# A two-layer hybrid decoder trunk on one core: the first weight splits cut in two, the opening loads re-gated, and layer 1's squares added up on GpSimd

## The chip, the cores and the metric

The kernel runs on one core of a Trainium2 chip. The metric is device time in microseconds (us) of one execution. The core's engines run side by side and are named here as in the profile: PE is TensorE (matrix multiplications; PEld its weight loads), DVE is VectorE, ACT is ScalarE, POOL is GpSimd, SP is SyncE, which issues most of the loads and stores. Matmul results land in PSUM; everything else lies in SBUF, 128 partitions wide.

## What is computed

The reference carries a residual stream of 528 tokens (16 learned meta tokens, then 512 positions) by 1024 features through two layers, all in float32. Cut to what matters here:

```python
for l in range(DEPTH):                       # DEPTH = 2
    h = rmsnorm(h_res, norm_gain[l])
    proj = h @ w_in[l]
    u_pool, z_pool, c_q, c_kv, k_rope, z_mla, g_pool, g_mla = jnp.split(proj, IN_SPLIT_POINTS, axis=-1)
    y_pool = (pool_mix(u_pool, pool_w_group[l], pool_scale[l]) * jax.nn.silu(z_pool)) @ pool_w_up[l]
    o_mla = mla(c_q, c_kv, k_rope, pos, ...)           # c_q and c_kv are RMS-normed again; 8 heads, causal
    y_mla = (o_mla * jax.nn.silu(z_mla)) @ mla_w_up[l]
    merged = jax.nn.sigmoid(g_pool) * y_pool + jax.nn.sigmoid(g_mla) * y_mla
    h_res = h_res + merged @ w_out[l]
```

`rmsnorm` divides each token by the root of the mean of its squares over the 1024 features and multiplies each feature by a gain.

## The kernel before

**Layout.** Features lie on partitions and tokens along the free dimension, so the residual stream is eight tiles `xb[:, k]` of 128x528, k = 0 to 7. A product runs over the eight tiles as eight K steps, in two column halves of 264 tokens (`FULL`) in layer 0. In layer 1, whose meta tokens are needed only as keys and values, most products run over the 512 tokens at once (`XTOK`).

**Precision.** Each float32 operand is split into a rounded high part and a low remainder, and a product is three matmuls (`mm3`, L184 to L187): high weight by high data, high weight by low data, low weight by high data. For data the split is `split_h` (L333): ScalarE writes the high part `hh` with the norm's gain as scale (L337), VectorE the low part `hl` (L339). For weights it is `wload` (L170): a chunk of 128x512 (four K steps of 128 columns) comes into `raw`; ScalarE writes `whi` (L180), VectorE `wlo` (L181). The helper `split` (L275) does the same pair of instructions on any column range. The norm's division isn't in these operands: it is applied after the product, when the result leaves PSUM, with factors that are computed meanwhile.

**Norm sums.** `square_x` (L342) has ScalarE square each x tile (L344): in layer 0 after the first products, and in layer 1 for tile m as soon as layer 0's last product has written that tile (`ev_o`, L893, whose eviction is L903). `norm_sums` (L348) lets TensorE add these up across partitions with a matrix of ones, 32 columns wide: eight squares of x and two of the latent c_kv, by two column halves (L356). Four such matmuls stand side by side in the array, in four groups of 32 columns; x squares go alternately to two of them, and two partial sums come out, which are added after a trip through DRAM.

**Order of the work.** `register` (L914) lists the products of a layer in order: two of c_kv first, then c_q, u, keys and so on to the output product `o0` to `o7`. `stream` (L193) turns the list into chunks of 512 weight columns, with three to four loaded ahead, and exchanges the second and third chunk, so that the first four are: c_kv 0 K steps 0 to 3, c_kv 1 K steps 0 to 3, c_kv 0 K steps 4 to 7, c_kv 1 K steps 4 to 7. `step` (L238) advances it by a few matmuls, and `go` (L978) strings the layer together from such steps. The program's instructions are placed on the engines by a scheduler at compile time; each engine then runs its own list in order. `behind(a, b)` (L279) makes instruction a wait for b.

**The start.** The first chunk's load is issued on ScalarE's queue (L121) and named `first`. SP issues, in order, the norm scales `gn` (L122, 24 KB), x tile 0 (L123, 264 KB), the second chunk (L124, 256 KB) and x tile 1 (L125). `other_loads` (L141), called after tile 0's split, has SP load the rest behind `first`: x tiles 2 and 3 in one transfer (528 KB), the third chunk, tiles 4 and 5, the fourth chunk, tiles 6 and 7, the constants and the positions; weight chunks from the fifth on follow on the same queue (L114). Eight warm-up matmuls on a matrix of ones (L136) run on TensorE meanwhile. In `go`, layer 0 begins with this loop:

```python
for k in range(8):
    if k in (0, 1, 3, 5):
        step()                    # loads and splits the next chunk
    self.split_h(k)
    if k == 0:
        other_loads(first)
```

**The layer boundary.** `hh` and `hl` of layer 1 use the buffers that hold layer 0's merged result, the operand of `o0` to `o7`, so they are written while the last of these products finish. GpSimd has no work there; its next is an add for c_q (L563).

Of the kernel before, what the change touches and what calls it, by code (L numbers as in the profile page):

```python
# [9 lines left out]
F32 = mybir.dt.float32  # L10
# [3 lines left out]
AF = mybir.ActivationFunctionType  # L14
# [4 lines left out]
P = 128  # L19
# [4 lines left out]
T = SEQ + NM  # L24
# [11 lines left out]
MT_CKV = 0  # L36
# [35 lines left out]
def trunk(ctx, tc, xT, pos, win, wkr, wqb, wkb, wvb, wgr, wpu, wmu, wout, gains, const, yT):  # L72
# [45 lines left out]
        return wp.tile([P, 512], F32, tag="raw", name=nm("raw"), bufs=3)  # L118

    early.append(slot("rinv"))  # L120
    first = act.dma_start(early[0][:, 0:512], win[0, MT_CKV, :, 0:512])  # L121
    sp.dma_start(gn, gains)  # L122
    sp.dma_start(xb[:, 0, :T], xT[:, 0, :])  # L123
    early.append(fetch(win[0, MT_CKV + 1, :, 0:512], 512, rawt(), sp))  # L124
    sp.dma_start(xb[:, 1, :T], xT[:, 1, :])  # L125
# [13 lines left out]
    identr = cp.tile([P, P], F32R, name="identr")  # L139

    def other_loads(made):  # L141
        for k, m in ((2, 0), (4, 1), (6, None)):
            ins = sp.dma_start(xb[:, k:k + 2, :T], xT[:, k:k + 2, :])
            behind(ins, made)
            if m is not None:
                raw = rawt()
                behind(sp.dma_start(raw, win[0, MT_CKV + m, :, 512:1024]), made)
                early.append(raw)
        behind(sp.dma_start(cst, const), made)
        behind(sp.dma_start(posb[:, :T], pos.partition_broadcast(P)), made)  # L150
        dve.tensor_copy(maskw[:, 512 - P:], cst[:, C_MASK:C_MASK + P])
        dve.tensor_copy(identr, ident)
# [13 lines left out]
            self.spare = False  # L166

    loads = [0]

    def wload(src, n, gain, spare):  # L170
        raw = early.pop(0) if early else fetch(src, n, rawt(), sp)
        loads[0] += 1
        pool, th, tl, nb = (tp, "th", "tl", 2) if loads[0] <= 2 or spare else (wp, "whi", "wlo", 3)
        if gain is not None:
            v = raw[:, :n].rearrange("p (k m) -> p k m", k=8)
            gp.tensor_mul(v, v, gain.unsqueeze(2).to_broadcast([P, 8, n // 8]))
            return raw, None
        hi = pool.tile([P, W if pool is tp else 512], F32R, tag=th, name=nm("whi"), bufs=nb)
        lo = pool.tile([P, W if pool is tp else 512], F32R, tag=tl, name=nm("wlo"), bufs=nb)
        act.activation(hi[:, :n], raw[:, :n], AF.Copy)  # L180
        dve.tensor_sub(lo[:, :n], raw[:, :n], hi[:, :n].bitcast(F32))  # L181
        return hi, lo

    def mm3(out, wh, wl, xh, xl, start, stop):  # L184
# [94 lines left out]
    def behind(ins, other):  # L279
        tc.add_manual_dep(ins.ins, other.ins.name,  # L280
                          mybir.DependencyInfo(mybir.DependencyClass.Sync, mybir.DependencyReason.DATA))
# [32 lines left out]
    class Layer:  # L314
# [18 lines left out]
        def split_h(self, k):  # L333
            gk, x = self.g(G_H + k), self.xt[k]
            hh, hl = self.hs[k]
            for a, b in FULL if (self.l, k) == (0, 0) else [(0, T)]:
                made = act.activation(hh[:, a:b], x[:, a:b], AF.Copy, scale=gk)  # L337
                self.made[k] = self.made[k] or made
                dve.scalar_tensor_tensor(out=hl[:, a:b], in0=x[:, a:b], scalar=gk, in1=hh[:, a:b].bitcast(F32),  # L339
                                         op0=ALU.mult, op1=ALU.subtract)  # L340

        def square_x(self, k):  # L342
            self.xsq[k] = slot(f"cq{4 + k}" if k < 4 else f"q{k}")
            made = act.activation(self.xsq[k][:, :T], self.xt[k][:, :T], AF.Square)  # L344
            if self.l == 0:
                behind(made, self.made[min(k + 3, 7)])

        def norm_sums(self):  # L348
            fill_now(2600)
            px, pc = mmt(), mmt()  # L350
            runs = [(px, self.xsq[k], k, k < 2, k >= 6) for k in range(8)] + [(pc, self.csq[m], m, True, True) for m in range(2)]
            for k in range(0, 10, 2):
                for s, (a, b) in enumerate(FULL):
                    for ps, t, m, start, stop in runs[k:k + 2]:
                        g = 64 * s + 32 * (m % 2)
                        mm = pe.matmul(ps[g:g + 32, :HALF], ones[:, 0:32], t[:, a:b], start=start, stop=stop,  # L356
                                       tile_position=(0, g))
                        if t is not self.csq[1]:
                            behind(mm, self.csq_last)
            sums = tmp()  # L360
            for s, (a, b) in enumerate(FULL):
                act.activation(sums[0:64, a:b], px[64 * s:64 * s + 64, :HALF], AF.Copy)
                dve.tensor_copy(sums[64:128, a:b], pc[64 * s:64 * s + 64, :HALF])
            raw, norms = nsr[self.l], ndr[self.l]
            sp.dma_start(raw, sums[0:97:32, 0:T])
            C = T // 16
            parts = lambda d: d.rearrange("i (s c) -> s i c", c=C)
            fill_now(2600)
            nq = sm.tile([16, 4, C], F32, tag="nq", name=nm("nq"))
            na, nt, ny = (sm.tile([16, n, C], F32, tag=t, name=nm(t)) for t, n in (("na2", 2), ("nt2", 2), ("ny2", 3)))  # L370
            sp.dma_start(nq, parts(raw))
            dve.tensor_scalar(na[:, 0, :], nq[:, 0, :], 1.0 / D, EPS, op0=ALU.mult, op1=ALU.add)
            dve.scalar_tensor_tensor(out=na[:, 0, :], in0=nq[:, 1, :], scalar=1.0 / D, in1=na[:, 0, :],
                                     op0=ALU.mult, op1=ALU.add)
            dve.tensor_scalar(na[:, 1, :], na[:, 0, :], EPS, None, op0=ALU.mult)
            dve.tensor_scalar(ny[:, 2, :], na[:, 1, :], EPS, None, op0=ALU.mult)
            for m in range(2):
                dve.scalar_tensor_tensor(out=na[:, 1, :], in0=nq[:, 2 + m, :], scalar=1.0 / 256,
                                         in1=na[:, 1, :], op0=ALU.mult, op1=ALU.add)
            newton(ny[:, 0:2, :], na, nt)  # L380
            sp.dma_start(parts(norms), ny)
            self.inv, self.cinv = slot("rinv"), slot("q1")
            if self.l == 0:
                tables()
            fill_now(RET)
            for i, d in enumerate((self.inv, self.cinv)):
                behind(sp.dma_start(d[:, 0:T], norms[i:i + 1, :].partition_broadcast(P)), newest[0])
            self.st = [sct(), sct()]
# [589 lines left out]
        def go(self, nxt):  # L978
            l = self.l
            up = lambda name: upto((l, name))  # L980
            if l == 0:
                for k in range(8):
                    if k in (0, 1, 3, 5):
                        step()
                    self.split_h(k)
                    if k == 0:
                        other_loads(first)
            up("ckv1")
            if l == 0:
                for k in range(8):  # L990
                    self.square_x(k)
            self.norm_sums()
            up("u1")
            self.ninv = self.columns(1)
            for m in range(2):
                self.mix(m, self.window(m))
            up("u3")
            s2 = self.window(2)
            up("k3")
            s3 = self.window(3)  # L1000
            up("zp0")
            self.mix(2, s2)
            up("zp1")
            self.mix(3, s3)
            self.k_factors()
            self.eps = self.columns(2)
            up("qr1")
            for s, (a, b) in enumerate(FULL):
                a0 = max(a, self.x0)
                self.stat(self.acc[:, a0:b], a0, b, C_CQ, self.acc_last)  # L1010
            up("qn3")
            self.qk_stats()
            fill_now(2600)
            kq = self.prep(0)
            fill_now(2600)
            due[0] = None
            prev = None
            for h in range(H):
                kn_ = self.head(h, kq, prev)
                self.gap()  # L1020
                if h + 1 < H:
                    kq = self.prep(h + 1)
                self.pv(prev, (2, 3))
                prev = kn_
                self.gap()
            fill_now(1300)
            self.pv(prev, (0, 1))
            fill_now(2600)
            if not self.last:
                self.meta_queries()  # L1030
            self.pv(prev, (2, 3))
            up("gm7")
            flush()
            if not self.last:
                for p in range(4):
                    self.meta_out(p)
            up("o7")
            if nxt is not None:
                for k in range(8):
                    nxt.split_h(k)  # L1040
# [76 lines left out]
```

## Time and profile before

| | us |
|---|---|
| median of three timed runs | 787.66 |
| lowest and highest of them | 787.45, 788.19 |
| the profiled execution | 787.15 |
| its span in the profile | 785.4 |
| TensorE busy | 779.9 |
| VectorE busy | 536.7 |
| ScalarE busy | 410.9 |
| GpSimd busy | 195.5 |

The profile is of one execution. Its span runs from the first to the last instruction of the core; its time holds 1.75 us more, ahead of and behind the span. The granted clock of TensorE is 1.0 of full speed over the whole span. In rows of the timeline the first number is the start in us, the second the time until the end of the last instruction of the row (with xN for several); a bracket tells how long the engine stood idle before it and what ended that. Matmuls are pipelined, so one that takes 0.28 us may be followed by the next 0.12 us later. In rows that group instructions, the numbers behind the first bar are the total busy time in us and the mean of one in ns. A row of waits names who waited for whom, the total, how often, and the longest. A row of DMA issues ends with the median time from issue to landing.

### The profile page before, as it was taken

The numbers are of one execution on the slowest core, as the hardware profiler recorded it, in microseconds if no ns is written. First come the engines' busy times: TensorE is split into PE (matmuls) and PEld (weight loads), VectorE is DVE, ScalarE is ACT, GpSimd is POOL, SyncE is SP. The second block draws the span as 40 slices with busy tenths as digits, with TensorE's granted clock in tenths as the row PEclk, the third lists the DMA queues.
The fourth block names the chain that finished last, engine by engine and source line by source line (L and its number), as shares of the span: only waits on it lengthen the run. The fifth ranks groups of instructions, "written<-read, shape, count | busy, mean of one in ns | idle before, by whom it ended". The sixth has DMA issues, their size and how long they took to land.

```text
span 785.4 us, 14564 instructions
## 1 busy us (share of the span) xinstructions
PE 779.9 (99%) x5291; PEld 708.0 (90%) x5291; DVE 536.7 (68%) x1163; ACT 410.9 (52%) x930; POOL 195.5 (25%) x259
## 2 busy tenths in 40 slices
PE   9999999999999999999999999999999999999998
PEld 8999899999999999999997898887788888887887
DVE  5768778357779987685355577774477888755932
ACT  7645655555656565633354356455456666554421
POOL 1033504012333242052000235130132333410600
DMA  7233333323333222325642322434242323222372
GB/s 243 83 102 87 95 120 102 115 83 102 90 86 89 74 63 81 96 81 143 183 136 94 104 82 86 124 99 138 70 129 88 95 84 84 62 81 67 98 241 90
DMA packets 52983, 81.88 MB, mean 104 GB/s; under 512 B 9496, under 2 KB 18072, under 8 KB 52912
## 3 DMA queue, kind: packets, MB, share of 16 engines
q1 hardware_dynamic: 52768, 80.70, 33.8%
q8 instruction: 41, 0.67, 0.4%
q14 instruction: 30, 0.25, 0.1%
q10 hardware_dynamic: 144, 0.26, 0.1%
HBM read 74.51 MB, written 4.29 MB: 100 GB/s over the span
## 4 chain that ended last, share of the span: by engine, by line
PE 97%; DMA 1%; DVE 1%; ACT 0%; issue 0%; ACTq 0%
PE mm L185 29%; PE mm L187 28%; PE mm L186 28%; PE mm L801 2%; PE S L186 2%; PE S L187 2%; PE S L185 1%; PE o L807 1%; PE o L806 1%; PE S L456 1%; DMA xb<-xT 1%; PE mm L356 1%; PE mm L415 0%; DMA rinv<-win 0%; DMA raw<-wmu 0%; PE mm L812 0%
## 5 line engine op out<-in xcount | busy, mean ns | idle before, releaser
L185 PE MATMUL mm<-hh,whi 128*128 128x264 f32 (+2 forms) x1096 | 346.1, 317 | 0.5 <-ACT whi L180 0.3
L186 PE MATMUL mm<-hl,whi 128*128 128x264 f32 (+2 forms) x1096 | 343.7, 315 | 0.0
L187 PE MATMUL mm<-hh,wlo 128*128 128x264 f32 (+2 forms) x1096 | 342.6, 315 | 0.0
L181 DVE TENSOR_TENSOR wlo<-raw,whi 128x512 fp32r<-128x512 f32 (+2 forms) x251 | 188.7, 755 | 114.1 <-ACT whi L180 110.4
L180 ACT ACTIVATE whi<-raw 128x512 fp32r<-128x512 f32 (+2 forms) x251 | 150.1, 601 | 186.3 <-PE mm L186 129.8
L185 PEld LDWEIGHTS mm<-hh,whi 128*128 128x128 f32 x1096 | 205.7, 188 | 14.0 <-ACT racc L815 0.5
L186 PEld LDWEIGHTS mm<-hl,whi 128*128 128x128 f32 x1096 | 206.4, 188 | 11.8
L187 PEld LDWEIGHTS mm<-hh,wlo 128*128 128x128 f32 x1096 | 205.4, 188 | 12.1
L563 POOL TENSOR_TENSOR racc<-racc,tmp 128x264 f32<-128x264 f32 (+1 forms) x15 | 14.6, 978 | 151.7 <-ACT tmp L562 151.7
L704 POOL TENSOR_TENSOR tmp<-kp,bc 64x528 f32<-64x528 f32 x16 | 24.2, 1512 | 105.5 <-issue 90.0
L779 POOL TENSOR_TENSOR pm<-pa,rs 128x16 f32<-128x16 f32 x32 | 11.6, 361 | 149.8 <-DVE rs L774 149.8
L889 POOL TENSOR_TENSOR tmp<-tmp,xb 128x264 f32<-128x264 f32 (+1 forms) x24 | 27.0, 1150 | 58.5 <-DVE tmp L887 32.3
L735 DVE CUSTOM_DVE_ANT_0 S<-S,maskw,nqs 128x272 f32<-128x272 f32 (+4 forms) x80 | 38.4, 498 | 2.3 <-PE S L187 1.9
L742 ACT ACTIVATE cq<-S,bia 128x400 f32<-128x400 f32 (+2 forms) x48 | 24.6, 515 | 21.4 <-DVE bia L769 11.7
L185 PE MATMUL mm<-u,whi 128*128 128x264 f32 (+1 forms) x108 | 35.3, 327 | 0.0
L187 PE MATMUL mm<-u,wlo 128*128 128x264 f32 (+1 forms) x108 | 34.7, 321 | 0.0
L187 PE MATMUL mm<-cq,wlo 128*128 128x264 f32 (+1 forms) x108 | 34.6, 322 | 0.0
L185 PE MATMUL mm<-cq,whi 128*128 128x264 f32 (+1 forms) x108 | 34.6, 320 | 0.0
L186 PE MATMUL mm<-cq,whi 128*128 128x264 f32 (+1 forms) x108 | 34.5, 321 | 0.0
L277 DVE TENSOR_TENSOR tl<-mm,th 128x512 fp32r<-128x512 f32 (+1 forms) x64 | 29.2, 481 | 7.0 <-ACT th L276 6.3
L781 POOL TENSOR_TENSOR cq<-cq,rs 128x384 f32<-128x384 f32 (+1 forms) x32 | 33.0, 1030 | 0.0
L276 ACT ACTIVATE th<-mm 128x512 fp32r<-128x512 f32 (+1 forms) x64 | 25.4, 433 | 10.7 <-PE mm L801 10.4
(246 smaller groups left out, 1363.6 us busy)
## 6 DMA issues: line engine op xcount, KB each, us to landing
raw<-win SPq DMA_DIRECT2D x143, 256.0 KB, 2.6
raw<-wout SPq DMA_DIRECT2D x32, 256.0 KB, 3.1
bc<-kdr SPq DMA_DIRECT2D x16, 264.0 KB, 3.6
raw<-wpu SPq DMA_DIRECT2D x16, 256.0 KB, 2.7
raw<-wmu SPq DMA_DIRECT2D x16, 256.0 KB, 2.7
raw<-wqb SPq DMA_DIRECT2D x12, 256.0 KB, 2.6
tmp<-xT SPq DMA_DIRECT2D x16, 132.0 KB, 3.2
tmp<-scr SPq DMA_DIRECT2D x7, 256.0 KB, 3.0
```

Of the source, the lines that this page charges most:

```text
L180: act.activation(hi[:, :n], raw[:, :n], AF.Copy)
L181: dve.tensor_sub(lo[:, :n], raw[:, :n], hi[:, :n].bitcast(F32))
L185: pe.matmul(out, wh, xh, start=start, stop=False)
L186: pe.matmul(out, wh, xl, start=False, stop=False)
L187: newest[0] = pe.matmul(out, wl, xh, start=False, stop=stop)
L276: act.activation(hi[:, a:b], src, AF.Copy)
L277: dve.tensor_sub(lo[:, a:b], src, hi[:, a:b].bitcast(F32))
L704: gp.tensor_mul(kf[r0:r0 + 64, :], self.kp[r0:r0 + 64, :], bc[r0:r0 + 64, :])]
L735: dve.tensor_tensor_reduce(out=sv, in0=sv, in1=mask, scale=nqs[:, i, h:h + 1], scalar=3e38, op0=ALU.add, op1=ALU.min, accum_out=bia[:, c:c ...
L742: act.activation(pv, sv, AF.Exp, scale=-1.0, bias=bia[:, i:i + 1], accum_out=rs[:, c:c + 1])
L781: gp.tensor_mul(pt[i][:, NM:], pt[i][:, NM:], rs[:, i:i + 1].to_broadcast([P, n - NM]))
L889: gp.tensor_add(t[:, :b - a], t[:, :b - a], self.am[m][:, a:b])
```

## The change

- The first chunk's load is no longer the gate of the other loads; the load of the norm scales `gn` is.
- `other_loads` issues x tiles 2 to 7 one by one, with the third chunk behind tile 3 and the fourth behind tile 4.
- Of the first two chunks, `wload` splits columns 0 to 127 (K step 0) at once; the other 384 columns are split by a function kept in `rests`. That of the first chunk is called behind tile 0's split, that of the second behind tile 1's, and ScalarE's part of each waits for the high part of that tile (`made`, which now holds the last of the tile's two halves).
- In layer 1, `square_x` has GpSimd add up the squares: behind an odd tile the pair, behind tiles 3 and 7 the two pairs as well. The sums of tiles 0 to 3 and 4 to 7 lie in the first and fifth tile, and `norm_sums` takes these two in place of eight.

```diff
--- before.py
+++ after.py
@@ -118,8 +118,8 @@
         return wp.tile([P, 512], F32, tag="raw", name=nm("raw"), bufs=3)
 
     early.append(slot("rinv"))
-    first = act.dma_start(early[0][:, 0:512], win[0, MT_CKV, :, 0:512])
-    sp.dma_start(gn, gains)
+    act.dma_start(early[0][:, 0:512], win[0, MT_CKV, :, 0:512])
+    first = sp.dma_start(gn, gains)
     sp.dma_start(xb[:, 0, :T], xT[:, 0, :])
     early.append(fetch(win[0, MT_CKV + 1, :, 0:512], 512, rawt(), sp))
     sp.dma_start(xb[:, 1, :T], xT[:, 1, :])
@@ -139,12 +139,11 @@
     identr = cp.tile([P, P], F32R, name="identr")
 
     def other_loads(made):
-        for k, m in ((2, 0), (4, 1), (6, None)):
-            ins = sp.dma_start(xb[:, k:k + 2, :T], xT[:, k:k + 2, :])
-            behind(ins, made)
-            if m is not None:
+        for k in range(2, 8):
+            behind(sp.dma_start(xb[:, k, :T], xT[:, k, :]), made)
+            if k in (3, 4):
                 raw = rawt()
-                behind(sp.dma_start(raw, win[0, MT_CKV + m, :, 512:1024]), made)
+                behind(sp.dma_start(raw, win[0, MT_CKV + k - 3, :, 512:1024]), made)
                 early.append(raw)
         behind(sp.dma_start(cst, const), made)
         behind(sp.dma_start(posb[:, :T], pos.partition_broadcast(P)), made)
@@ -166,6 +165,7 @@
             self.spare = False
 
     loads = [0]
+    rests = []
 
     def wload(src, n, gain, spare):
         raw = early.pop(0) if early else fetch(src, n, rawt(), sp)
@@ -177,8 +177,14 @@
             return raw, None
         hi = pool.tile([P, W if pool is tp else 512], F32R, tag=th, name=nm("whi"), bufs=nb)
         lo = pool.tile([P, W if pool is tp else 512], F32R, tag=tl, name=nm("wlo"), bufs=nb)
-        act.activation(hi[:, :n], raw[:, :n], AF.Copy)
-        dve.tensor_sub(lo[:, :n], raw[:, :n], hi[:, :n].bitcast(F32))
+        first = P if loads[0] <= 2 else n
+        split(hi, lo, raw[:, 0:first], 0, first)
+        if first < n:
+            def rest(made):
+                behind(act.activation(hi[:, first:n], raw[:, first:n], AF.Copy), made)
+                dve.tensor_sub(lo[:, first:n], raw[:, first:n], hi[:, first:n].bitcast(F32))
+
+            rests.append(rest)
         return hi, lo
 
     def mm3(out, wh, wl, xh, xl, start, stop):
@@ -335,7 +341,7 @@
             hh, hl = self.hs[k]
             for a, b in FULL if (self.l, k) == (0, 0) else [(0, T)]:
                 made = act.activation(hh[:, a:b], x[:, a:b], AF.Copy, scale=gk)
-                self.made[k] = self.made[k] or made
+                self.made[k] = made
                 dve.scalar_tensor_tensor(out=hl[:, a:b], in0=x[:, a:b], scalar=gk, in1=hh[:, a:b].bitcast(F32),
                                          op0=ALU.mult, op1=ALU.subtract)
 
@@ -344,12 +350,19 @@
             made = act.activation(self.xsq[k][:, :T], self.xt[k][:, :T], AF.Square)
             if self.l == 0:
                 behind(made, self.made[min(k + 3, 7)])
+                return
+            for w in (1, 2):
+                if k % (2 * w) == 2 * w - 1:
+                    d, e = self.xsq[k - 2 * w + 1], self.xsq[k + 1 - w]
+                    gp.tensor_add(d[:, :T], d[:, :T], e[:, :T])
 
         def norm_sums(self):
             fill_now(2600)
             px, pc = mmt(), mmt()
-            runs = [(px, self.xsq[k], k, k < 2, k >= 6) for k in range(8)] + [(pc, self.csq[m], m, True, True) for m in range(2)]
-            for k in range(0, 10, 2):
+            xs = self.xsq[::4] if self.l else self.xsq
+            runs = [(px, t, m, m < 2, m >= len(xs) - 2) for m, t in enumerate(xs)]
+            runs += [(pc, t, m, True, True) for m, t in enumerate(self.csq)]
+            for k in range(0, len(runs), 2):
                 for s, (a, b) in enumerate(FULL):
                     for ps, t, m, start, stop in runs[k:k + 2]:
                         g = 64 * s + 32 * (m % 2)
@@ -982,9 +995,13 @@
                 for k in range(8):
                     if k in (0, 1, 3, 5):
                         step()
+                        if k == 1:
+                            rests.pop(0)(self.made[k - 1])
                     self.split_h(k)
                     if k == 0:
                         other_loads(first)
+                    if k == 1:
+                        rests.pop(0)(self.made[k])
             up("ckv1")
             if l == 0:
                 for k in range(8):
```

## The prediction

> **What bounds the kernel now.** I read the page first (busy time, and the shares of the chain that ended last), then what TensorE waits for, then that chain's first pieces in order of time, and last the two places that the diff touches.
>
> ```profile
> PE 779.9 (99%) x5291; PEld 708.0 (90%) x5291; DVE 536.7 (68%) x1163; ACT 410.9 (52%) x930; POOL 195.5 (25%) x259
> ...
> PE 97%; DMA 1%; DVE 1%; ACT 0%; issue 0%; ACTq 0%
> ```
> ```profile
> PE wps L136 <- DVE na L680: 1.0, 1, 1.0
> PE mm L185 <- ACT whi L180: 0.3, 1, 0.3
> ```
> ```profile
> 0.73 2.86 DMA rinv<-win
> 3.61 5.02 DMA xb<-xT
> 8.65 0.74 ACT hh L337
> 9.42 0.78 DVE hl L339
> 10.24 0.39 PE S L186
> ```
>
> The reader sees that TensorE is the bound: 779.9 us busy of a span of 785.4, 97% of the chain, and behind the first wait (1.0 us, ahead of the warm-up matmuls) none above 0.3 us. So time is won in two ways only: fewer matmuls, or an earlier moment from which TensorE never stands still. The chain names that moment. Ahead of 10.24 us it is not TensorE's: the first weight chunk lands at 3.59, this releases the load of x tiles 2 and 3, which lands at 8.63; ScalarE rounds tile 2, VectorE forms its low part until 10.20, and from 10.24 on it is matmuls.
>
> **The change part by part.** *Norm sums of layer 1.*
>
> ```profile
> 420.60 1.10 PE L356 MATMUL mm<-cq,ones 128*32 128x264 f32 x16
> ...
> 421.52 1.52 PE L356 MATMUL mm<-q,ones 128*32 128x264 f32 x24
> ...
> 422.96 0.50 PE L185 MATMUL mm<-hh,whi 128*128 128x512 f32 x1
> ```
>
> Ten tensors (eight squares of x, two of c_kv) by two column halves are 20 matmuls; the trace has 40 instructions, two to a matmul. They hold TensorE from 420.60 to 422.96: 2.36 us, 0.059 us an instruction. With four squares added up in each of two tensors, (2 + 2) x 2 x 2 = 16 instructions are left, in groups of four as before: 16 x 0.059 = 0.94 us. This takes 24 x 0.059 = **1.42 us** out of TensorE's queue where TensorE is the bound, so all of it counts. Layer 0 keeps its 40.
>
> What is added for it are six adds of 128x528 on GpSimd: one behind the square of tile 1, two behind tile 3's, one behind tile 5's, two behind tile 7's.
>
> ```profile
> L522 POOL TENSOR_TENSOR tmp<-u 128x542 f32<-128x542 f32 x3 | 4.7, 1563 | 6.3 <-DVE u L499 6.3
> ...
> L522 POOL TENSOR_TENSOR tmp<-u 128x528 f32<-128x528 f32 x1 | 1.1, 1066 | 0.9 <-DVE u L499 0.9
> ```
> ```profile
> 404.84 0.63 ACT L344 ACTIVATE q<-xb 128x528 f32<-128x528 f32 x1
> ```
> ```profile
> 431.60 1.33 POOL L563 TENSOR_TENSOR racc<-racc,tmp 128x512 f32<-128x512 f32 x1 [72.32 <-ACT tmp L562]
> ```
>
> By these rows an add costs 1.07 to 1.56 us, six 6.4 to 9.4. GpSimd has stood idle for 72 us when it starts at 431.60, so nothing waits behind the adds on its queue. The last square ends at 405.47, the two adds behind it by 407.6 to 408.6, and TensorE wants them at 420.60: 12 us of cover. I cost them at nothing; without that cover it would be the last two, 2.1 to 3.1 us. GpSimd may also slow VectorE beside it:
>
> ```profile
> 403.83 0.43 DVE L903 SCALAR_TENSOR_TENSOR xb<-mm,tmp 128x264 f32<-128x264 f32 x1
> ...
> 407.49 0.69 DVE L181 TENSOR_TENSOR wlo<-raw,whi 128x512 fp32r<-128x512 f32 x1
> ```
> ```profile
> 397.73 0.28 PE L185 MATMUL mm<-hh,whi 128*128 128x264 f32 x1
> ...
> 403.46 0.28 PE L187 MATMUL mm<-hh,wlo 128*128 128x264 f32 x1
> ```
>
> Between the last two rows lie 47 steps from matmul to matmul, so one takes 0.122 us. VectorE evicts layer 0's last tile at 403.83. TensorE then has two chunks of 24 matmuls (5.9 us, to about 409.6) before it needs the two chunks that VectorE finishes at 408.18. VectorE may thus slip 1.4 us at no cost.
>
> The Trainium skill (GPSIMD Engine Reference, § 1 and § 4.1) speaks against this part: an elementwise add of two inputs belongs on VectorE, as GpSimd is about twice as slow and shares its SBUF interface with VectorE's instructions that have two SBUF inputs. Where that would lead here is the third rival, priced from rows.
>
> *The start.*
>
> ```profile
> 1.18 0.41 SPq L123 DMA_DIRECT2D xb<-xT  x1
> ```
> ```profile
> 1.05 3.78 PE L136 MATMUL wps<-ones 128*128 128x128 f32 x16 [1.05 <-DVE na L680]
> ...
> 4.34 0.92 ACT L337 ACTIVATE hh<-xb,gn 128x264 fp32r<-128x264 f32 x2
> ...
> 5.77 0.63 ACT L180 ACTIVATE whi<-raw 128x512 fp32r<-128x512 f32 x1 [0.51 <-DMA raw<-win]
> ...
> 6.43 0.74 ACT L337 ACTIVATE hh<-xb,gn 128x528 fp32r<-128x528 f32 x1
> ...
> 7.20 0.77 DVE L339 SCALAR_TENSOR_TENSOR hl<-xb,gn,hh 128x528 fp32r<-128x528 f32 x1
> ...
> 13.82 1.36 ACT L337 ACTIVATE hh<-xb,gn 128x528 fp32r<-128x528 f32 x2
> ...
> 14.58 1.45 DVE L339 SCALAR_TENSOR_TENSOR hl<-xb,gn,hh 128x528 fp32r<-128x528 f32 x2 [0.52 <-ACT hh L337]
> ```
> ```profile
> xb<-xT SPq DMA_DIRECT2D x3, 528.0 KB, 5.0
> xb<-xT SPq DMA_DIRECT2D x2, 264.0 KB, 3.1
> ```
> ```profile
> 2.00:11.60 9.60, 9.01 (x53) 7.91 (x52) 5.02 (x8) 6.51 (x12) 1.62 (x6) 1.00 0.97 335
> 6.00:8.00 2.00, 1.72 (x14) 1.52 (x12) 1.46 (x2) 1.13 (x2) 0.00 (x0) 1.00 1.05 322
> 9.00:18.00 9.00, 8.76 (x70) 8.35 (x69) 6.52 (x11) 9.00 (x17) 0.00 (x0) 1.00 0.68 258
> 12.00:14.00 2.00, 2.00 (x18) 2.00 (x18) 2.00 (x5) 2.00 (x5) 0.00 (x0) 1.00 1.02 394
> ```
>
> (In the windows the last two columns are the DMA engines' busy share and GB/s, the one ahead the granted clock.) The two splits: ScalarE takes 0.46 us for a half of 264 columns (0.92 x2) and 0.74 for 528, so 0.0011 us a column; 128 columns cost about 0.3 us and the other 384 about 0.5, VectorE's pieces the same. Each chunk costs both engines 0.1 to 0.2 us more in all and frees its first piece 0.35 us sooner. For the first chunk that frees nothing: x tile 0 lands at 1.18 + 3.1 = 4.28 by a load that stays where it is, ScalarE begins it at 4.34 either way, and the warm-up matmuls hold TensorE until 4.83. The second chunk lands near 5.72 as now, so its matmuls begin at about 6.1 in place of 6.45. Tile 1 has landed by 6.43, as ScalarE goes straight on to it. I put it at 6.35: ScalarE has it by 7.1 and the second chunk's rest by 7.6, VectorE tile 1's low part by 7.9 and that rest by 8.45, and the 24 matmuls of tiles 0 and 1 are done at about 8.75.
>
> The other loads wait for the scales, not for the weight chunk at 3.59. No row shows the scales land. They are 24 KB, issued at 0.74 ahead of tile 0, which took 3.1 us with eleven times the bytes, and are used at 4.34; I take 3.2. The issue itself is worth little, from -0.2 to 0.4 us, as the DMA engines are 0.97 busy from 2.0 us on. What counts is that tile 2 no longer comes as one load with tile 3. Its 264 KB are 270 thousand bytes, at 322 GB/s 0.84 us: it lands at 8.63 - 0.84 = 7.8, with the issue's gain at 7.4. Three more DMA issues (0.41 us the row above) lengthen SP's queue by 1.2 us; behind them stand the constants, the positions and the fifth weight chunk, whose matmuls come behind 96 others (11.7 us): covered.
>
> With tile 2 at 7.7, ScalarE has it by 8.45 and VectorE its low part by 9.25. TensorE does its 24 matmuls until 8.75, four with tile 2's high part until 9.24, and then takes the low part, where it stood at 10.24 before: 1.0 us. By the load alone it is 0.84, and if tile 2 comes sooner still, tile 1's chain (8.75) holds it at 1.0. I take **0.9 us**. What is late next is ScalarE, busy throughout from 9 to 18 us: it rounds tiles 6 and 7 from 13.82 on, tile 6's low part is there at 14.58 + 0.73 = 15.3, and TensorE asks for it 48 matmuls behind 10.24, at 16.1. So 0.8 us are safe even if ScalarE's late tiles don't move; third and fourth chunk stand one tile earlier in the queue. Lower end 0.2, if squares are put ahead of tiles; upper end 1.6, if tile 1 comes sooner too.
>
> **The sum.** The profiled execution took 787.15 us, 785.4 of span and 1.75 around it: 787.15 - 1.42 - 0.9 = 784.83. The median of the three timed runs is 787.66, 0.51 higher; 787.66 - 2.32 = **785.3**. A difference of 0.2%, 1.6 us, is about what a measurement of this kernel can tell from no change.
>
> **The rivals.** (1) *The start gives little or nothing*: single loads move slower, or ScalarE's new order takes back what tile 2 gives. Against it: from 12 to 14 us, with the pairs through (9.6 us x 335 GB/s is 3.2 million bytes by 11.6 us, the last x tile among them), single loads run at 394 GB/s, the pairs' time has 322. For it: the compiled order of ScalarE's work is in no trace of before, and one square is 0.63 us. Only the norm sums stay: 787.66 - 1.42 = 786.2. Chance 0.18. The Trainium skill (DMA: Bandwidth & Descriptors, § Bandwidth) weighs on this side: it advises batches of 1 MiB or more. The windows just read don't agree for loads that overlap.
>
> (2) *A better start*: tile 1 lands sooner too, and the gain is 1.3 to 1.6 us: 784.7. Against it: its load stands where it did. Chance 0.1.
>
> (3) *GpSimd holds VectorE off at the layer boundary.* If the two exclude each other, VectorE slips by the last two adds, 2.1 to 3.1 us, of which 1.4 are covered: TensorE stalls 0.7 to 1.7, 786.0 to 787.0. For it: the splits stand right there. Against it: adds of this size differ by 0.5 us at most, so engines that meet slow each other by less than an instruction. Chance 0.06.
>
> (4) *Slower: the engines serve all loads in flight in parallel.* Then tile 2, released together with five tiles and two chunks, doesn't go first. At the worst all land together: their bytes have moved by 11.6 us, and landing comes some 1.3 later (the pair's 1.6 million bytes had moved by about 7.2 at 322 GB/s, and it landed at 8.63), at 12.9. TensorE starts 4.2 us later than now: 787.66 + 4.2 - 1.42 = 790.4. The point from which it decides is tile 2 landing later than 8.63 + 1.42 = 10.05. Against it: tile 0 landed at 4.28 with two later loads under way. Chance 0.06, as 788 to 790.5.
>
> **How the numbers follow.** The forecast has 0.6 (its own range 785.0 to 785.7), the rivals 0.18, 0.1, 0.06 and 0.06; predicted 785.3. Down to (2), up through (1) and part of (3), the range is 784.4 to 786.6. Faster by over 0.2% (below 786.1): the forecast, (2) and a bit under half of (1), 0.78. Within 0.2%: the rest of (1), (3) and a little of (4), 0.16. Slower: most of (4), 0.06.
>
> **What would show it.** Right would be: 16 matmul instructions in layer 1's norm sums, 0.94 us; six GpSimd adds ahead of 409 us and no TensorE wait for them; tile 2's rounding at 7.5 to 7.9 in place of 8.65; its first low-part matmul near 9.3, with no TensorE gap behind. Wrong would be a tile 2 that lands after 8.6, gaps of TensorE from 10 to 18 us, or a wait at the layer boundary.

## The result, and the profile after

The changed kernel takes 785.63 us (median of 12 runs, 785.29 to 787.55) against 787.43 for the kernel before (12 runs, 786.61 to 788.19): a ratio of 0.9979, interval 0.9972 to 0.9986, so 1.8 us less. Its profiled execution took 785.55 us with a span of 783.8; that of before had 787.15 and 785.4.

The page of the changed kernel, busy times and then the shares of the chain that ended last:

```profile
PE 778.4 (99%) x5267; PEld 707.5 (90%) x5267; DVE 541.0 (69%) x1165; ACT 411.0 (52%) x932; POOL 204.8 (26%) x265
...
PE 98%; DMA 1%; DVE 0%; ACT 0%; issue 0%; SPq 0%; ACTq 0%
```

TensorE has 24 instructions fewer and is still the bound. GpSimd is busy 9.3 us more, and VectorE 4.3 us more although it has only two short instructions more: something slows it. The changed kernel's chain, its first pieces in order of time:

```profile
0.74 0.39 SPq L122
1.19 3.14 DMA xb<-xT
4.42 0.52 ACT hh L343
4.98 1.00 PE S L191 x2
5.98 0.22 PE S L192
...
23.93 2.36 PE mm L369 x40
```

(The chain puts the start of layer 0's norm sums at 23.93 us, the end of the piece ahead of them; their first instruction starts at 23.86. By the same two readings the kernel before has 24.65 and 24.58. The expectations below were written with the first, the tables with the second.) Before, the chain went through tile 2's load, ScalarE and VectorE until 10.24 us. Now it is TensorE's from 4.98 us on, and ahead of that only tile 0's load and rounding stand on it. TensorE's waits in the changed kernel, the two longest:

```profile
PE wps L136 <- DVE na L693: 1.1, 1, 1.1
PE mm L191 <- ACT q L282: 0.3, 1, 0.3
```

The wait for tile 2 is gone and none has come in its place. Where the gain stands, read at the same instruction of both traces:

| event | before, us | after, us | gain |
|---|---|---|---|
| first matmul of layer 0's norm sums | 24.58 | 23.86 | 0.72 |
| last eviction of layer 0 | 403.83 | 403.32 | 0.51 |
| first matmul of layer 1's norm sums | 420.60 | 420.09 | 0.51 |
| first product behind them | 422.96 | 421.12 | 1.84 |
| last output eviction | 782.37 | 780.51 | 1.86 |
| end of the span | 785.4 | 783.8 | 1.6 |

So the start gave 0.72 us and the norm sums 1.33; 0.21 was lost between the layers' sums and 0.26 behind the last eviction.

The start, ScalarE's timeline of the changed kernel:

```profile
4.42 0.92 ACT L343 ACTIVATE hh<-xb,gn 128x264 fp32r<-128x264 f32 x2 [0.45 <-DMA xb<-xT]
5.56 0.31 ACT L282 ACTIVATE whi<-raw 128x128 fp32r<-128x128 f32 x1 [0.22 <-DMA raw<-win]
5.77 0.51 ACT L184 ACTIVATE whi<-rinv 128x384 fp32r<-128x384 f32 x1
6.23 1.41 ACT L343 ACTIVATE hh<-xb,gn 128x528 fp32r<-128x528 f32 x2
```

Tiles 1 and 2 stand in one row without a gap: tile 2 was there by 6.9 us (6.23 and half of the 1.41), and its rounding began then, where it began at 8.65 before. TensorE's timeline beside it:

```profile
5.78 0.42 PE L192 MATMUL S<-hl,whi 128*128 128x264 f32 x1
6.00 0.42 PE L193 MATMUL S<-hh,wlo 128*128 128x264 f32 x1
...
6.88 0.41 PE L192 MATMUL S<-hl,whi 128*128 128x264 f32 x1
7.10 0.31 PE L193 MATMUL S<-hh,wlo 128*128 128x264 f32 x1
7.24 0.29 PE L192 MATMUL mm<-hl,whi 128*128 128x264 f32 x1
7.37 0.41 PE L193 MATMUL mm<-hh,wlo 128*128 128x264 f32 x2
```

From start to start a matmul of 264 columns takes 0.22 us until 7.1 us and 0.12 to 0.13 behind it. This is not waiting: the rows have no bracket. The column of the granted clock reads 1.00 in these windows all the same. Layer 1's norm sums on TensorE:

```profile
420.09 0.41 PE L369 MATMUL mm<-cq,ones 128*32 128x264 f32 x1
...
420.36 0.83 PE L369 MATMUL mm<-q,ones 128*32 128x264 f32 x9
421.12 0.51 PE L191 MATMUL mm<-hh,whi 128*128 128x512 f32 x1
```

Sixteen instructions in 1.03 us in place of forty in 2.36. What was added for them, on GpSimd (the second fence is an answer to a window that ends between the last two adds):

```profile
405.04 4.28 POOL L357 TENSOR_TENSOR q<-q,q 128x528 f32<-128x528 f32 x2 [11.33 <-ACT q L350]
```
```profile
368.98 1.32 POOL L357 TENSOR_TENSOR cq<-cq,cq 128x528 f32<-128x528 f32 x1 [10.19 <-ACT cq L350]
...
405.04 2.53 POOL L357 TENSOR_TENSOR q<-q,q 128x528 f32<-128x528 f32 x1 [11.33 <-ACT q L350]
```

An add by itself takes 1.32 us; the last two take 2.53 and 1.75. VectorE beside them:

```profile
406.30 1.83 DVE L345 SCALAR_TENSOR_TENSOR hl<-xb,gn,hh 128x528 fp32r<-128x528 f32 x1
408.06 1.81 DVE L283 TENSOR_TENSOR wlo<-raw,whi 128x512 fp32r<-128x512 f32 x1
```

The same two took 0.76 and 0.69 us before. So the adds do hold VectorE off, by 2.2 us, and TensorE shows no wait for it.

### The profile page after: what moved, and what is told of

Read it like the earlier page. It is cut to its first block, busy times and chain, and to the rows that moved or that the text cites. A ratio compares the mean times of both kernels' runs of the same rounds, so it can differ in the third digit from the quotient of the medians.

```text
span 783.8 us, 14539 instructions
## 1 busy us (share of the span) xinstructions
PE 778.4 (99%) x5267; PEld 707.5 (90%) x5267; DVE 541.0 (69%) x1165; ACT 411.0 (52%) x932; POOL 204.8 (26%) x265
## 4 chain that ended last, share of the span: by engine, by line
PE 98%; DMA 1%; DVE 0%; ACT 0%; issue 0%; SPq 0%; ACTq 0%
PE mm L191 29%; PE mm L193 28%; PE mm L192 28%; PE mm L814 2%; PE S L191 2%; PE S L192 2%; PE S L193 2%; PE o L820 1%; PE o L819 1%; PE S L469 1%; PE mm L428 0%; PE mm L369 0%; DMA xb<-xT 0%; DMA raw<-wmu 0%; PE mm L825 0%; PE mm L842 0%
## 5 line engine op out<-in xcount | busy, mean ns | idle before, releaser
L283 DVE TENSOR_TENSOR wlo<-raw,whi 128x512 fp32r<-128x512 f32 (+2 forms) x251 | 190.7, 763 | 113.8 <-ACT whi L282 110.1
L192 PE MATMUL mm<-kn,whi 128*128 128x264 f32 (+1 forms) x96 | 30.6, 321 | 0.0
```

The lines of the kernel that those rows point to most:

```text
L192: pe.matmul(out, wh, xl, start=False, stop=False)
L283: dve.tensor_sub(lo[:, a:b], src, hi[:, a:b].bitcast(F32))
```

## The experiments

My theory: two separate gains, 1.42 us from the norm sums and 0.9 from the start, the latter because tile 2 no longer shares a load with tile 3. The rivals: the gate alone makes the start; the pieces matter; GpSimd's adds cost something at the boundary; without a gate it would be the same. All differences below are medians against the kernel before, measured beside it (12 runs of it for the changed kernel, 27 to 33 for the others, with medians of 787.24 to 787.72 us); the experiments have 11 runs each, e6_pairs 7 and e9_adds3 one. The ratio, with its interval, is estimated apart from the medians and can differ from their quotient: for e10_gate it stands for 0.4 us, the medians for 0.73. "Sums 0" is the start of layer 0's norm sums; "full pace" is the first matmul from which TensorE goes by 0.12 us. Both are read from one execution each.

| kernel | us | against before | ratio, interval | sums 0 | full pace |
|---|---|---|---|---|---|
| before (profile) | | | | 24.58 | 5.9 |
| changed (profile) | 785.63 | -1.80 | 0.9979, 0.9972 to 0.9986 | 23.86 | 7.1 |
| e1_sums | 786.31 | -1.41 | 0.9983, 0.9975 to 0.9992 | 24.60 | 5.65 |
| e2_start | 786.89 | -0.83 | 0.9989, 0.998 to 0.9998 | 23.68 | 6.2 |
| e3_loads | 786.90 | -0.82 | 0.9992, 0.9983 to 1.0001 | 23.82 | 5.6 |
| e4_pieces | 787.77 | +0.05 | 0.9998, 0.999 to 1.0007 | 24.69 | 5.7 |
| e5_gate_back | 785.88 | -1.48 | 0.9981, 0.9972 to 0.999 | 24.05 | 6.45 |
| e6_pairs | 785.17 | -2.19 | 0.9976, 0.9964 to 0.9987 | 23.61 | 6.7 |
| e7_nowarm | 786.19 | -1.17 | 0.9983, 0.9974 to 0.9992 | 23.91 | 9.5 |
| e8_l0adds | 785.89 | -1.47 | 0.9979, 0.997 to 0.9987 | 25.38 | |
| e10_gate | 786.51 | -0.73 | 0.9995, 0.9986 to 1.0003 | 23.55 | 5.6 |
| e11_nogate | 785.74 | -1.50 | 0.9981, 0.9972 to 0.9989 | 24.33 | 6 to 6.8 |
| e12_again | 785.48 | -1.76 | 0.9978, 0.9969 to 0.9987 | 23.46 | 5.6 |

e9_adds3 has one time, 785.25 us.

**The two halves (e1_sums, e2_start).** On the kernel before, the first has only the adds and the shorter sums, the second all but these:

```diff
+            for w in (1, 2):
+                if k % (2 * w) == 2 * w - 1:
+                    d, e = self.xsq[k - 2 * w + 1], self.xsq[k + 1 - w]
+                    gp.tensor_add(d[:, :T], d[:, :T], e[:, :T])
...
+            xs = self.xsq[::4] if self.l else self.xsq
...
```

> Only the second part of the change: GpSimd adds layer 1's squares and the norm sums take two tensors in place of eight; the start is that of before. Theory: TensorE's queue is 24 instructions shorter at a place where it is the bound, so the time falls by 1.42 us (1.3 to 1.5) and the norm sums of layer 1 hold TensorE for 0.94 to 1.05 us in place of 2.36. Rival (GpSimd holds VectorE off at the layer boundary, TensorE pays): less than 0.9 us of it is left, and TensorE shows a wait between 404 and 413 us.

> Only the first part: the gate on the norm scales, tiles 2 to 7 as single loads, the first two chunks split in pieces; the norm sums are those of before. Theory: the moment from which TensorE never stands still comes earlier, layer 0's norm sums begin near 23.9 us in place of 24.65, and the time falls by 0.5 to 0.9 us; with the sums alone this adds up to the whole change. Rival (the two parts share a gain or hinder each other): the two parts alone add up to more or less than the whole by over 0.5 us.

Measured: -1.41 and -0.83 us. In e1_sums the sums of layer 0 start where they did (24.60) and those of layer 1 are over in 1.02 us, and TensorE shows no wait from 395 to 425 us; in e2_start layer 0's start 0.90 earlier. The two parts are separate; their sum, -2.24, is no further from the whole's -1.80 than the three intervals allow.

**The start taken apart (e3_loads, e4_pieces, e10_gate).** On the kernel before: e3_loads has the new gate and single loads, without the pieces; e4_pieces has only the pieces; e10_gate only this:

```diff
-    first = act.dma_start(early[0][:, 0:512], win[0, MT_CKV, :, 0:512])
-    sp.dma_start(gn, gains)
+    act.dma_start(early[0][:, 0:512], win[0, MT_CKV, :, 0:512])
+    first = sp.dma_start(gn, gains)
```

> Of the start only the loads: the gate on the norm scales and single loads of tiles 2 to 7; the first two chunks are split whole, the norm sums are those of before. Theory: it was the load of tiles 2 and 3 that TensorE waited for, so most of the start's gain is here: tile 2's rounding starts by 7.4 us in place of 8.65, layer 0's norm sums begin 0.4 to 0.8 us earlier. Rival (the pieces bring the gain, the loads don't): the norm sums begin within 0.15 us of 24.65.

> Of the start only the pieces: the first two chunks are split in 128 columns and the rest; loads, gate and norm sums are those of before. Theory: TensorE's wait for tile 2 swallows what it wins ahead of it, so layer 0's norm sums begin within 0.15 us of 24.65 and the time is that of before. Rival (the pieces bring the gain): the norm sums begin 0.4 us earlier or more.

> The kernel before with the gate alone moved to the norm scales: pairs of tiles, whole splits, eight squares in both layers. Theory, as formed on the runs so far (released 0.3 us earlier, the loads reach the engines before the first four run dry near 5 us; single loads are not needed): the moved bytes stay near 350 GB/s or more from 5 to 6 us, tile 2's rounding starts by 7.6 us in place of 8.65, layer 0's norm sums begin at 23.7 to 24.0 us. Rival (the gate is worth no more than the 0.3 us by which it opens earlier): tile 2's rounding starts at 8.3 us or later and the norm sums at 24.3 or later.

The times alone (-0.82, +0.05, -0.73) hardly tell these apart, as all three intervals reach past 1. The traces do: layer 0's sums start 0.76 and 1.03 us earlier with e3_loads and e10_gate, and 0.11 later with e4_pieces. Tile 2 in e4_pieces, from its chain, and in e10_gate, from ScalarE's timeline:

```profile
3.69 4.76 DMA xb<-xT
```
```profile
7.49 0.74 ACT L337 ACTIVATE hh<-xb,gn 128x528 fp32r<-128x528 f32 x1 [0.58 <-DMA xb<-xT]
```

With the old gate the pair is issued at 3.69 and lands at 8.45; with the new one the same pair is there by 7.49, a microsecond sooner, from a gate that opens 0.32 us earlier (SP issues it at 3.37 in e10_gate). The windows of the two, last columns DMA share and GB/s, hint at why; e4_pieces, then e10_gate:

```profile
5.00:6.00 1.00, 0.97 (x5) 0.78 (x6) 0.99 (x3) 1.00 (x4) 0.00 (x0) 1.00 0.73 253
```
```profile
5.00:6.00 1.00, 1.00 (x4) 0.70 (x4) 0.87 (x3) 0.84 (x2) 0.00 (x0) 1.00 1.13 425
```

In e4_pieces the DMA engines have a hollow from 5 to 6 us; with the new gate it is filled. It would be the time in which the first batch of loads has moved and the second has not begun: the five loads ahead of the gate are 1.09 million bytes, and by 5 us 1.04 million have moved (the windows from 1 to 5 us have 23, 211, 401 and 404 GB/s). That this hollow makes the whole of the microsecond isn't shown: the profile of before has no such dip, only 288 to 326 GB/s throughout from 4 to 9 us, and a pair as late.

**Gate and pairs, each put back (e5_gate_back, e6_pairs, e11_nogate).** From the changed kernel: e5_gate_back takes the old gate, e6_pairs loads tiles 2 to 7 in pairs again, and e11_nogate has pairs that wait for no gate at all. The edit of e6_pairs:

```diff
-        for k in range(2, 8):
-            behind(sp.dma_start(xb[:, k, :T], xT[:, k, :]), made)
+        for k, m in ((2, 0), (4, 1), (6, None)):
+            ins = sp.dma_start(xb[:, k:k + 2, :T], xT[:, k:k + 2, :])
+            behind(ins, made)
...
```

> The changed kernel with the gate put back: the loads of tiles 2 to 7 wait for the first weight chunk again, still one by one. Theory (the single loads bring the gain, the gate little): layer 0's norm sums begin within 0.3 us of the changed kernel's 23.93, and tile 2's rounding starts before 7.8 us. Rival (the gate brings it, by keeping the queue full from 3.4 us on): tile 2's rounding starts at 8.2 us or later, the norm sums at 24.3 or later, and 0.4 us or more of the gain is gone.

> The changed kernel with tiles 2 to 7 loaded in pairs again, behind the norm scales. Theory (single loads bring the gain): tile 2 waits for tile 3 again and its rounding starts at 7.8 us or later; 0.4 us or more of the start's gain is gone. Rival (the gate brings it): layer 0's norm sums begin within 0.2 us of 23.93.

> The changed kernel with tiles 2 to 7 in pairs and no gate at all: the loads are issued right behind the first four, from 2.6 us on. Theory (the engines take the loads in the order of issue): tile 0 still lands near 4.33, the second chunk by 5.6, and the norm sums of layer 0 begin within 0.25 us of 23.67, as TensorE's slow pace is the limit by now. Rival (loads in flight share the engines): tile 0 or the second chunk lands 0.3 us later or more, and the first matmuls and the norm sums move back by as much.

Measured: -1.48, -2.19 and -1.50 us. With pairs and the new gate nothing is lost: sums 0 at 23.61. ScalarE of e6_pairs, tiles 2 and 3 without a wait:

```profile
7.30 1.37 ACT L344 ACTIVATE hh<-xb,gn 128x528 fp32r<-128x528 f32 x2
```

With the old gate and single loads, tile 2 (chain of e5_gate_back) lands at 7.45, sooner than the 7.8 that I had worked out for single loads by themselves, and sums 0 is at 24.05:

```profile
3.68 3.77 DMA xb<-xT
```

So either edit brings tile 2 about a microsecond sooner: it lands at 8.45 to 8.63 with neither, at 7.45 with single loads, by 7.30 to 7.49 with the new gate, and by 6.9 with both. Sums 0 doesn't follow all the way. With the old gate and single loads TensorE goes on to tile 2 at 8.27, right behind its rounding, 0.3 us later than it could; once the gate is moved, single loads give TensorE nothing over pairs. Without any gate the second weight chunk pays; ScalarE's timeline of e11_nogate:

```profile
6.26 0.31 ACT L283 ACTIVATE whi<-raw 128x128 fp32r<-128x128 f32 x1 [0.93 <-DMA raw<-win]
```

It begins at 6.26, where all the kernels with a gate have 5.2 to 5.8 (the changed one 5.56), and sums 0 slips to 24.33. By this one execution loads issued later delay this earlier one; tile 0, ahead of it, still lands in time for 4.41.

**The slow pace (e7_nowarm, e12_again).** e7_nowarm is the changed kernel without the warm-up matmuls; e12_again is the changed kernel once more. The edit of e7_nowarm:

```diff
-WARM = 8
+WARM = 0
```

> The changed kernel without the eight warm-up matmuls. Theory: what limits the start now is no load but TensorE's own pace, 0.22 us from matmul to matmul until 7.1 us and 0.12 from then on; without earlier matmuls the slow pace lasts until some 8.4 to 11.8 us (3.4 us more of work), and the time rises by 0.6 to 2.2 us against the changed kernel. Rival (loads and splits limit the start, the slow pace hides beside them): the time stays within 0.3 us of the changed kernel's.

> The changed kernel itself once more, beside the others on one chip. Theory: it stands 1.4 to 2.1 us below the kernel before; its slow pace at the start ends at another moment than in its first profile (7.1 us), and layer 0's norm sums begin the earlier the sooner it ends, between 23.6 and 24.0. Rival (the moment is fixed by the program): it ends at 7.1 us again.

TensorE of e7_nowarm, then of e12_again:

```profile
9.28 0.42 PE L193 MATMUL S<-hh,wlo 128*128 128x264 f32 x1
9.50 0.34 PE L191 MATMUL S<-hh,whi 128*128 128x264 f32 x1
9.68 0.28 PE L191 MATMUL mm<-hh,whi 128*128 128x264 f32 x1
9.80 0.28 PE L192 MATMUL mm<-hl,whi 128*128 128x264 f32 x1
```
```profile
4.98 0.80 PE L191 MATMUL S<-hh,whi 128*128 128x264 f32 x2 [0.21 <-ACT hh L343]
5.62 0.28 PE L192 MATMUL S<-hl,whi 128*128 128x264 f32 x1
5.74 0.28 PE L193 MATMUL S<-hh,wlo 128*128 128x264 f32 x1
```

Without warm-up the slow pace lasts until 9.5 us and the kernel takes 0.6 us more than with it. (The compiled order is another there, with some eight matmuls fewer ahead of layer 0's sums, so its 23.91 doesn't compare; layer 1's sums start at 420.86, 0.77 later than in the changed kernel.) One and the same program went slowly until 7.1 us in one execution and until 5.6 in the other, with sums 0 at 23.86 and 23.46: the moment of full pace isn't the program's. The Trainium skill (TensorE: Matmul & The Clock Gate, Part 1) has the array run at half rate until it has been busy for one window of about 3.4 us, and the window runs free of the program, so that the moment varies from run to run. The traces agree: 0.22 against 0.12 us, and two executions of one program in which the moment differs by 1.5 us, more than the half microsecond either way that the page gives.

The 0.40 us between their sums 0, though, is hardly the pace's. ScalarE and TensorE of e12_again, then VectorE and TensorE of the changed kernel's first profile:

```profile
5.24 0.29 ACT L282 ACTIVATE whi<-raw 128x128 fp32r<-128x128 f32 x1
5.86 1.35 ACT L343 ACTIVATE hh<-xb,gn 128x528 fp32r<-128x528 f32 x2
```
```profile
7.43 0.39 PE L192 MATMUL S<-hl,whi 128*128 128x264 f32 x1 [0.18 <-DVE hl L345]
```
```profile
7.00 1.45 DVE L345 SCALAR_TENSOR_TENSOR hl<-xb,gn,hh 128x528 fp32r<-128x528 f32 x2
```
```profile
7.86 0.36 PE L192 MATMUL S<-hl,whi 128*128 128x264 f32 x1
```

In e12_again TensorE, at full pace by then, stands until VectorE has tile 1's low part and takes it at 7.43. In the first profile the second weight chunk came later: ScalarE began it 0.32 us later (5.56, behind a wait for its load) and tile 1 0.37 later (6.23), VectorE had tile 1's low part at about 7.75, and TensorE, at the slow pace until shortly before, took it at 7.86. Layer 0's sums follow 16.0 us behind that matmul in both. So tile 1's low part, and ahead of it the second chunk's load, sets the start in both executions; a faster pace could have won 0.1 us at most in the first.

**GpSimd's adds (e8_l0adds, e9_adds3).** e8_l0adds is the changed kernel with layer 0's squares added up too, each add put behind the last low part. In e9_adds3 the last two adds run three times each, so that the squares of tiles 4 to 7 enter layer 1's norm sums several times over. The edit of e9_adds3:

```diff
-                    gp.tensor_add(d[:, :T], d[:, :T], e[:, :T])
+                    for _ in range(3 if k == 7 else 1):
+                        gp.tensor_add(d[:, :T], d[:, :T], e[:, :T])
```

> The changed kernel with layer 0's squares added up on GpSimd as well, the adds held back until the last tile's split is done (about 15 us). Theory: layer 0's norm sums fall from 40 to 16 instructions, another 1.42 us, if six adds of 1.3 us or more fit between 15 us and the sums at 23.9; they take 7.9 us without company, so it is tight: TensorE waits 0 to 1.2 us, and the time falls by 0.2 to 1.4 us against the changed kernel. Rival (the adds meet VectorE's work, 2.1 us each as the last two of layer 1): they end near 27 us and the kernel is slower than the changed one.

> The changed kernel with each of the two adds behind tile 7's square done three times, so that GpSimd works for about 9 to 13 us at the layer boundary in place of 4.3. The computation is changed by it: in layer 1 the squares of tiles 4 to 7 enter the norm with wrong weights. Theory (what hides GpSimd's hold on VectorE is that TensorE needs VectorE's last chunk only near 412 us, and the sums at 420): VectorE's evictions of c_kv, from 411 us on, now meet the adds as well, but TensorE waits less than 0.5 us. Rival (VectorE was at the edge): TensorE waits 1 us or more between 404 and 420 us, and the execution is longer by as much.

e9_adds3 took 785.25 us with a span of 783.4, no more than the changed kernel. GpSimd and VectorE in it:

```profile
404.67 10.71 POOL L358 TENSOR_TENSOR q<-q,q 128x528 f32<-128x528 f32 x6 [11.31 <-DMA raw<-win]
```
```profile
412.71 1.34 DVE L635 CAST pa<-kl 128x128 fp32r<-128x128 f32 x1
413.98 0.48 DVE L419 SCALAR_TENSOR_TENSOR kl<-mm,gn,kh 128x264 fp32r<-128x264 f32 x1
414.38 1.55 DVE L283 TENSOR_TENSOR wlo<-raw,whi 128x512 fp32r<-128x512 f32 x1
```

Adds that last until 415.4 still cost TensorE no wait. Most of VectorE's instructions whose operands are all in SBUF are slow beside them (the cast takes 0.22 us elsewhere; one split of a chunk at 412.11 has its usual 0.68), the one that reads PSUM is not. The Trainium skill (SBUF — State Buffer, SBUF: two separate sides) says that GpSimd and a VectorE instruction with two SBUF inputs, or in a mode that uses both ports, lock each other out of a shared pair of ports for a whole instruction. The 1.8 us of the two-input instructions agree with that; the cast has one input and is slow as well, and whether it ran in such a mode no run here shows.

e8_l0adds should have taken another 1.42 us out of TensorE's queue. It took 785.89, at the same ratio as the changed kernel (0.9979): nothing is won. VectorE's and TensorE's rows there:

```profile
19.57 1.83 DVE L283 TENSOR_TENSOR wlo<-raw,whi 128x512 fp32r<-128x512 f32 x1
21.32 1.34 DVE L635 CAST pa<-kl 128x128 fp32r<-128x128 f32 x1
22.58 0.48 DVE L419 SCALAR_TENSOR_TENSOR kl<-S,gn,kh 128x264 fp32r<-128x264 f32 x1
```
```profile
25.38 0.38 PE L370 MATMUL mm<-cq,ones 128*32 128x264 f32 x1 [1.23 <-ACT q L421]
```

The six adds are over in time, at 23.86 us. But VectorE's second step on c_kv (kl) starts at 22.58, in the changed kernel at 19.30, and its last ends at 24.8, there at 21.2; ScalarE's squares of c_kv come behind them, and TensorE stands for 1.23 us ahead of the sums. The same mechanism that is free at the layer boundary eats the gain here: the first product behind the sums starts at 26.61, in the changed kernel at 26.23.

## Why the prediction was right, and where not

Predicted were 785.3 us and a gain of 2.3; measured are 785.63 and 1.8, inside the range and inside the forecast's own 785.0 to 785.7.

**Norm sums: right, by the step given.** 1.42 predicted; 1.33 in the trace and -1.41 us with that part alone (e1_sums).

**The start: right in size, and only half right in the cause.** 0.9 predicted; 0.72 in the trace, 0.73 to 0.83 with the start or parts of it alone. Two steps fell: "What counts is that tile 2 no longer comes as one load with tile 3" and "The issue itself is worth little, from -0.2 to 0.4 us, as the DMA engines are 0.97 busy from 2.0 us on". The gate alone, with the load issued 0.32 us earlier, brings tile 2 a microsecond and layer 0's sums 1.03 us forward (e10_gate), and with it pairs are as good as single loads (e6_pairs). Single loads do what was said of them, but they aren't what counts: with the pieces, under the old gate, they bring 0.53 (e5_gate_back). The size came out all the same because of a bound that the prediction does name, tile 1's chain: it holds TensorE whichever edit brings tile 2. A mean over 9.6 us says nothing of the moments around the gate. But slices of a microsecond would not have given it away either: the profile of before has a DMA share of 0.97 at 288 GB/s from 4 to 5 us, and no hollow. Only the edit alone told.

**Tile 2 sooner than I said, and tile 1 the bound.** 7.4 to 7.8 us predicted, by 6.9 measured; its first low-part matmul was to be near 9.3 and, by the count of matmuls, starts at 9.16. That the sooner tile won no more fits "if tile 2 comes sooner still, tile 1's chain (8.75) holds it at 1.0": tile 1's low part was put at 7.9 and was there at about 7.75. But in the compiled order only 14 of the 24 matmuls of tiles 0 and 1 run ahead of it, so the 24 are done at 9.16 and not at 8.75, and the 29th matmul, which started at 10.24 before, starts at 9.64: 0.6 us were won there, not 1.0, and 0.72 by the sums. The slow pace, which I had not counted (eight matmuls from 4.98 to 7.10 us, 2.1 us, where e12_again needs 1.4), runs beside this chain; it becomes the bound when the warm-up is left out. The better start of rival (2) shows where the second chunk, and so tile 1, comes sooner: e12_again has sums 0 at 23.46, a gain of 1.12.

**The pieces: right that they free next to nothing.** +0.05 us alone, where the wait for tile 2 could have hidden a gain; but with the new loads too it is -0.83 with them (e2_start) and -0.82 without (e3_loads), so they give nothing that shows.

**GpSimd: free, as costed, but by a cover that I had sized wrongly.** "VectorE may thus slip 1.4 us at no cost": it slipped 2.2, which by these figures would have cost 0.8, and nothing came of it: the cost of nothing was right in part by luck. I had taken both chunks that VectorE finishes last to be due at 409.6. The last of them is c_kv 1's K steps 4 to 7, the fourth chunk in the order, due behind 72 matmuls: 403.3 + 72 x 0.122 = 412.1. It was ready at 409.87, 2.2 us early, so the cover was 4.4 us and not 1.4. Rival (3) thus had the mechanism (two engines that hold each other off by most of an instruction, which I had argued against with adds that "differ by 0.5 us at most") and the slip, and not the price; e8_l0adds shows the price where no cover is.

**The rest.** Three more DMA issues cost nothing that shows: the constants' load starts 1.0 us later and nobody waits for it. Something of rival (4) was seen, and only without a gate (e11_nogate). The 0.21 us lost between the two layers' sums is within what that stretch shows anyway: in the kernels with the same order of work it lasts from 395.9 to 396.5 us, with before at 396.0. The 0.26 behind the last eviction was not followed up.

**Open.** What makes the pair a microsecond sooner for 0.3 us of gate; whether single loads or pairs are better with the new gate (e6_pairs at 0.9976 and the changed kernel at 0.9978 and 0.9979 have intervals that overlap); how much of the differences of 0.1 to 0.4 us in sums 0 belongs to the second chunk's landing, which differs from execution to execution, and how much to the pace (in e6_pairs tile 1's low part is there at 7.50, and TensorE comes to it only at 7.91).

## What to carry to other kernels

Where loads are released in batches, a gate can be worth more than the time by which it opens sooner: try the gate alone, as the bytes moved around the release need not show it beforehand. Where TensorE is the bound, work moved from it to GpSimd is a full gain only if VectorE has slack at that place, and the slack is counted to the moment when its result is due, chunk by chunk. And take a start apart part by part: here three edits came together; by the traces the gate alone made the gain, single loads under the old gate brought about half of it, and the pieces none; the whole could not tell.

## What the runs showed of the hardware that I had not expected

- GpSimd and VectorE slow each other by most of an instruction (an add alone takes 1.32 us): 0.76 to 1.83 and 0.69 to 1.81 us on VectorE, 1.32 to 2.53 on GpSimd; a cast of one input too, 0.22 to 1.34; not an instruction that reads PSUM (0.48).
- TensorE's half pace at the start (0.22 against 0.12 us for 264 columns) does not show in the granted clock, and ended between 5.6 and 7.1 us in executions with the same warm-up.
- A load issued early came later with more loads in flight behind it: the second chunk's rounding at 6.26 us with the gate taken away, at 5.2 to 5.8 with one (one execution of each kernel).
- A pair of tiles released 0.32 us earlier landed a microsecond earlier (by 7.49 in place of 8.45 us).
